# Moving the start addresses of the weight buffers and the stationary activations by two paddings

## The chip, the cores and the metric

The kernel runs on one core of a Trainium2 chip. The metric is the device time of that core in microseconds. Before the change it is 2356.5 us, the median of 3 runs (2355.69 to 2361.19 us).

## The reference

The program is one inference step of a two-layer hybrid backbone (D_MODEL 2048) on two sequences of 128 tokens, a "prompt" and a "sample". Everything is float32. A layer does, cut to what matters here:

```python
h = rms_norm(x, norm_w) * (1 + scale) + shift          # shift, scale, gate = silu(c) @ w_mod + b_mod
(hg..., at..., s5_u, s5_g, merge_raw) = split_columns(h @ w_in)
o_hg = hgrn_branch(...)      # gated linear recurrence, chunkwise
o_at = block_attention(...)  # grouped-query attention
o_s5 = s5_branch(...)        # state space scan, then gelu(y), y * sigmoid(y @ w_glu)
merged = g_hg * (o_hg @ w_br_hg) + g_at * (o_at @ w_br_at) + g_s5 * (o_s5 @ w_br_s5)
x = x + gate * (merged @ w_out)
```

Nearly all the arithmetic is in the products with `w_in`, `w_br`, `w_out` and `w_glu`: for 256 rows (both sequences); the weights come in 672 pieces of 512 KB.

## The kernel before

**The big products.** `gemm` takes pieces of a weight matrix of 256 rows by 512 columns. Each piece lands by DMA (issued from SP) in one of three `raw` buffers. It holds two K-tiles of 128x512. Per K-tile ScalarE writes the rounded copy `wh` (line 138, type float32r) and VectorE the rest `wl = raw - wh` (line 139). Four `wh` and four `wl` buffers go round. The activations were split in the same way, once, into a high and a low part. For each K-tile and each of the two sequences TensorE then does three products into one PSUM tile `g`:

```python
nc.tensor.matmul(ps[s], lo(k)[:, sl], wh, start=(k == 0), stop=False)   # L178
nc.tensor.matmul(ps[s], hi(k)[:, sl], wh, start=False, stop=False)      # L179
nc.tensor.matmul(ps[s], hi(k)[:, sl], wl, start=False, stop=(k == nk - 1))  # L180
```

The activation block (128x128, 512 bytes in each partition) is the stationary operand, loaded into the array by a LDWEIGHTS (PEld). The weight tile (128x512, 2048 bytes in each partition) is the moving operand that streams through. So 1344 K-tiles make 8064 such products, and each of them has a load of its own stationary block.

**Where the operands lie.** The stationary parts have different names and homes. `hh` and `hl` (the normed input, for all of `w_in`) are in four buffers of the tag H8. `oh` and `ol` (outputs of the three branches, for `w_br`) are in two buffers of Z8. `ghl` (for `w_glu`) and one half of `mt` (merged, for `w_out`) are in S16; the other half of `mt` is in H8. The moving parts are always `wh` and `wl`. Every tile is written at a fixed byte address that is the same in all 128 partitions.

**What sets the addresses.** Three pools lie one behind the other: `const` (tables, in the order of their first use), `weights` (`raw`, `wh`, `wl`), and `sb` (all else: k2, Z8, sm, gt, mo, Bl, S16, ys, k4, H8, q4, kv, st and the small ones of the S5 branch). Within a pool each tag has its buffers in a row. A tile that grows by some bytes pushes all behind it up by so many. `c` (line 202) is the first tile of `const`; `bm` (line 251) is the only buffer of the tag mo, between gt and Bl.

**The order of the work.** A scheduler with priorities lays down each engine's list when the program is built. Side work (the S5 scan on VectorE, the `w_mod` products of line 273, attention and the recurrence) is mixed between the big products.

Of the kernel before, what the change touches and what calls it, by code (L numbers as in the profile page):

```python
# [57 lines left out]
def view(t, off, dims):  # L58
    return bass.AP(t.tensor, t.offset + off, [list(t.ap[0])] + [list(d) for d in dims])


class Builder:
# [136 lines left out]

    def condition(self):  # L200
        nc = self.nc
        c = self.const("c", (128, 32), src=self.io["cT"], eng=nc.scalar)
        self.cT = self.const("cs", (128, 64))
        nc.gpsimd.memset(self.cT, 0.0)
        sg = self.t2("sg", (128, 32))
        nc.scalar.activation(sg, c, AF.Sigmoid)
        nc.vector.tensor_mul(self.cT[:, 0:32], c, sg)
# [36 lines left out]
    def mod_part(self, l, part, prio, tags, plan):  # L244

        nc, io = self.nc, self.io
        with self.prio(prio):  # L250
            bm = self.t("mo", "bm", (128, 256))
            src = io["b_mod"][l, part]
            nc.gpsimd.dma_start(bm, bass.AP(src.tensor, src.offset, [[256, 4], [0, 32], [1, 256]]))
        kb = 0
        for bank, run, burst in plan:
            ps = None
            for k0 in range(kb, kb + run, burst):
                ws = []
                for k in range(k0, k0 + burst):
                    with self.prio(P_TOP):  # L260
                        tag, n = next(tags)
                        for i in range(0, 2, n):
                            w = self.t(tag if isinstance(tag, str) else tag[i], "wm", (128, n * 1024))
                            nc.sync.dma_start(w, io["w_mod"][l, part, k][:, i * 1024:(i + n) * 1024])
                            ws += [w[:, j * 1024:(j + 1) * 1024] for j in range(n)]
                with self.prio(prio):
                    if ps is None:
                        pool = dict(g=self.pg, m=self.pm, b=self.pb)[bank]
                        ps = pool.tile([128, 512], F32, tag=bank, name=self.nm("mod"))
                    for j, k in enumerate(reversed(range(2 * k0, 2 * (k0 + burst)))):  # L270
                        for i in range(4):
                            with self.prio(P_MIX if j + i else prio):
                                nc.tensor.matmul(ps[32 * i:32 * i + 32, 0:256], self.cT[:, 2 * k:2 * k + 32],  # L273
                                                 ws[k - 2 * k0][:, i * 256:i * 256 + 256], start=(k0 == kb and j == 0),
                                                 stop=(k0 + burst == kb + run and j == 2 * burst - 1),
                                                 tile_position=(0, 32 * i))
                    if k0 + burst == kb + run:
                        nc.vector.tensor_add(bm, bm, ps[:, 0:256])
                if k0 + burst < 8:
                    yield True  # L280
            kb += run
        with self.prio(P_CHAIN):
            if part >= 4:
                for i in range(4):
                    dst = bass.AP(self.gate_d.tensor, self.gate_d.offset + l * 2 * D + (part - 4) * 1024 + i * 256,
                                  [[D, 2], [1, 256]])
                    nc.gpsimd.dma_start(dst, bm[32 * i:32 * i + 2])
            else:
                tr = self.transpose4(bm, 2)
                mt = self.cp.tile([128, 2, 2, 4], F32, tag=f"modT{part}", name=self.nm("modT"))  # L290
                for s in range(2):
                    nc.vector.tensor_copy(view(mt, s * 4, [[8, 2], [2, 2], [1, 2]]),
                                          view(tr, s, [[64, 2], [32, 2], [128, 2]]))
                nc.vector.scalar_tensor_tensor(mt[:, 1], mt[:, 1], 1.0,
                                               view(self.normw, l * 16 + part * 4, [[0, 2], [1, 4]]), ALU.add, ALU.mult)
                self.mods[part] = mt
        yield True
# [910 lines left out]
```

## Time and profile before

| | |
|---|---|
| median of 3 runs | 2356.5 us |
| profiled execution | 2357.62 us, of which the span of the trace is 2355.8 us |
| TensorE matmul (PE) | busy 2290.3 us, 97% |
| weight load (PEld) | busy 1818.4 us, 77% |
| VectorE (DVE) | busy 1805.0 us, 77% |
| ScalarE (ACT) | busy 1180.3 us, 50% |
| DMA | 483.85 MB, mean 205 GB/s |
[...]

A matmul's own duration (about 0.39 us) is longer than the distance from its start to the next one's start, since matmuls are pipelined and their ends are modelled. What a stream of matmuls costs is therefore the time from the first start to the start of what follows, divided by their number.

### The profile page before, as it was taken

How to read it: one execution, taken by the hardware profiler on the slowest of the kernel's cores; microseconds unless marked ns; L12 is line 12 of the kernel's file. 1: busy time of each engine (PE TensorE's matmuls, PEld its weight loads, DVE VectorE, ACT ScalarE, POOL GpSimd, SP SyncE). 2: the span in 40 equal slices, each digit the busy share in tenths (PEclk: the TensorE clock that was granted, in tenths of full speed). 3: DMA queues.
4: the chain of work that ended last, by engine and by line, in shares of the span. 5: the costliest groups of instructions: out<-in, count | busy, mean ns of one | idle time of the engine just before them, and what ended most of it. 6: DMA issues, size and time to landing. Idle time of an engine off the chain costs nothing.

```text
span 2355.8 us, 38207 instructions
## 1 busy us (share of the span) xinstructions
PE 2290.3 (97%) x13192; PEld 1818.4 (77%) x13192; DVE 1805.0 (77%) x4835; ACT 1180.3 (50%) x2061; POOL 133.7 (6%) x244
## 2 busy tenths in 40 slices
PE   4999999999999999999989999999999999999997
PEld 2767877888887777777767888888878877887876
DVE  5855899799879868765565798899959959956555
ACT  3536645555554344544446555555564544554444
POOL 2000000100000100000010001000010010000000
PEclk8999999999999999999999999999999999999999
DMA  8994554345557878678873554444546577556665
GB/s 312 342 337 134 160 173 137 111 157 183 178 161 247 297 263 311 209 250 273 291 237 129 165 173 150 133 153 152 188 148 193 195 237 246 188 171 224 233 198 177
DMA packets 131490, 483.85 MB, mean 205 GB/s; under 512 B 17200, under 2 KB 17808, under 8 KB 126944
## 3 DMA queue, kind: packets, MB, share of 16 engines
q1 hardware_dynamic: 120528, 454.09, 57.1%
q0 software_dynamic: 9472, 23.97, 3.3%
q10 hardware_dynamic: 1296, 3.36, 0.4%
q8 instruction: 103, 1.69, 0.3%
q14 instruction: 91, 0.75, 0.1%
HBM read 474.36 MB, written 6.98 MB: 204 GB/s over the span
## 4 chain that ended last, share of the span: by engine, by line
PE 90%; DMA 5%; DVE 4%; issue 1%; ACT 1%; SPq 0%; DVEq 0%; ACTq 0%
PE g L178 25%; PE g L180 25%; PE g L179 25%; PE mod L273 3%; PE bu L815 2%; DMA wm<-w_mod 2%; PE lv L431 2%; PE tr L134 2%; DMA raw<-w_in 1%; PE yp L846 1%; DVE wl L139 1%; DMA raw<-w_br 1%; PE yp L839 1%; PE bt L733 1%; PE ao L571 0%
## 5 line engine op out<-in xcount | busy, mean ns | idle before, releaser
L138 ACT CAST wh<-raw 128x512 fp32r<-128x512 f32 x1344 | 819.1, 621 | 948.7 <-PE g L179 625.8
L139 DVE TENSOR_TENSOR wl<-raw,wh 128x512 fp32r<-128x512 f32 x1344 | 915.4, 689 | 382.2 <-ACT wh L138 345.0
L178 PE MATMUL g<-wh,hl 128*128 128x512 f32 x1984 | 794.4, 400 | 5.3 <-ACT wh L138 2.5
L179 PE MATMUL g<-wh,hh 128*128 128x512 f32 x1984 | 787.5, 397 | 0.0
L180 PE MATMUL g<-wl,hh 128*128 128x512 f32 x1984 | 709.8, 402 | 0.1
L178 PEld LDWEIGHTS g<-wh,hl 128*128 128x128 f32 x1984 | 375.0, 189 | 105.4 <-ACT wh L138 7.8
L179 PEld LDWEIGHTS g<-wh,hh 128*128 128x128 f32 x1984 | 375.2, 189 | 83.1 <-issue 0.2
L180 PEld LDWEIGHTS g<-wl,hh 128*128 128x128 f32 x1984 | 368.5, 189 | 87.7 <-DVE wl L139 2.9
L178 PE MATMUL g<-wh,ol 128*128 128x512 f32 x384 | 151.8, 395 | 0.8 <-ACT wh L138 0.6
L827 DVE TENSOR_TENSOR p<-s5sc,Sb 128x64 f32<-128x64 f32 x512 | 140.6, 275 | 15.0 <-ACT Sb L819 5.9
L179 PE MATMUL g<-wh,oh 128*128 128x512 f32 x384 | 150.0, 391 | 0.0
L833 DVE TENSOR_TENSOR Sb<-Sb,p 128x64 f32<-128x64 f32 x512 | 141.5, 276 | 8.9
L829 DVE TENSOR_TENSOR p<-s5sc,Sb 128x64 f32<-128x64 f32 x512 | 138.8, 271 | 0.0
L180 PE MATMUL g<-wl,oh 128*128 128x512 f32 x384 | 132.1, 393 | 0.0
L273 PE MATMUL mod<-wm,cs 128*32 128x256 f32 x1536 | 103.5, 401 | 24.9 <-DMA wm<-w_mod 18.5
L832 DVE TENSOR_TENSOR p<-p,p 128x64 f32<-128x64 f32 x512 | 113.3, 221 | 6.1
L273 PEld LDWEIGHTS mod<-wm,cs 128*32 128x32 f32 x1536 | 44.2, 113 | 76.0 <-DMA wm<-w_mod 23.7
L178 PE MATMUL g<-wh,mt 128*128 128x512 f32 x256 | 101.5, 397 | 0.0
L179 PE MATMUL g<-wh,mt 128*128 128x512 f32 x256 | 101.0, 394 | 0.0
L178 PEld LDWEIGHTS g<-wh,ol 128*128 128x128 f32 x384 | 72.1, 188 | 18.1 <-ACT wh L138 2.1
L180 PE MATMUL g<-wl,mt 128*128 128x512 f32 x256 | 84.7, 398 | 1.2 <-DVE wl L139 1.2
L180 PEld LDWEIGHTS g<-wl,oh 128*128 128x128 f32 x384 | 71.7, 188 | 16.6 <-DVE wl L139 0.8
(315 smaller groups left out, 2117.0 us busy)
## 6 DMA issues: line engine op xcount, KB each, us to landing
raw<-w_in SPq DMA_DIRECT2D x496, 512.0 KB, 3.6
wm<-w_mod SPq DMA_DIRECT2D x130, 512.0 KB, 7.1
raw<-w_br SPq DMA_DIRECT2D x96, 512.0 KB, 4.2
raw<-w_out SPq DMA_DIRECT2D x64, 512.0 KB, 4.3
wm<-w_mod SPq DMA_DIRECT2D x31, 1024.0 KB, 7.5
raw<-w_glu SPq DMA_DIRECT2D x16, 512.0 KB, 3.5
gb<-gate_d POOLq DMA_DIRECT2D x16, 256.0 KB, 5.9
x<-x ACTq DMA_DIRECT2D x2, 1024.0 KB, 14.5
```

Source lines behind the costliest of these rows:

```text
L134: nc.tensor.transpose(ps[:, k], src[:, k * 128:(k + 1) * 128], self.ident)
L138: self.nc.scalar.copy(hi, src)
L139: self.nc.vector.tensor_sub(lo, src, hi.bitcast(F32))
L178: nc.tensor.matmul(ps[s], lo(k)[:, sl], wh, start=(k == 0), stop=False)
L179: nc.tensor.matmul(ps[s], hi(k)[:, sl], wh, start=False, stop=False)
L180: nc.tensor.matmul(ps[s], hi(k)[:, sl], wl, start=False, stop=(k == nk - 1))
L273: nc.tensor.matmul(ps[32 * i:32 * i + 32, 0:256], self.cT[:, 2 * k:2 * k + 32], ws[k - 2 * k0][:, i * 256:i * 256 + 256], start=(k0 == kb ...
L431: nc.tensor.matmul(ps[:, h], mix[:, h], view(Z, HT + h * 128, [[2 * m, nb], [2 * HT + m, 2], [1, m]]), start=True, stop=True)
L827: tt(p0.rearrange("p d (j s) -> p d j s", s=2), view(sc, qd * 32, [[16, 2], [1, 16], [0, 2]]), view(Sb, i, [[ds, 2], [2 * W, 16], [W, 2]]) ...
L829: tt(p1, view(sc, 128 + qd * 64, [[32, 2], [16, 2], [1, 16]]), view(Sb, i + RI, [[ds, 2], [-RI, 2], [W, 16]]), ALU.mult)
L832: tt(p0, p0, p1, ALU.add)
L833: tt(cur, cur, p0, ALU.add)
```

## The change

Two tiles get wider, and only their first columns are used. `c` has 80 columns in place of 32, which is 192 bytes more; its load by DMA is written out on a line of its own. `bm` has 352 columns in place of 256, which is 384 bytes more. All tiles behind `c` move up by 192 bytes, all behind `bm` by 576.

```diff
     def condition(self):
         nc = self.nc
-        c = self.const("c", (128, 32), src=self.io["cT"], eng=nc.scalar)
+        c = self.const("c", (128, 80))[:, 0:32]
+        nc.scalar.dma_start(c, self.io["cT"])
         self.cT = self.const("cs", (128, 64))
...
         with self.prio(prio):
-            bm = self.t("mo", "bm", (128, 256))
+            bm = self.t("mo", "bm", (128, 352))[:, 0:256]
             src = io["b_mod"][l, part]
             nc.gpsimd.dma_start(bm, bass.AP(src.tensor, src.offset, [[256, 4], [0, 32], [1, 256]]))
```

The addresses of the two built programs, as bytes in a partition (the first buffer of each; a stationary block steps by 512 bytes within its tile, a buffer by 2048 or more, so the last two columns hold for every block of the row):

| tag | what | before | after | before mod 512 | after mod 512 |
|---|---|---|---|---|---|
| ident | identity, moving operand of the transposes | 16896 | 17088 | 0 | 192 |
| raw | weights as landed | 27968 | 28160 | 320 | 0 |
| wh, wl | moving operands | 40256, 48448 | 40448, 48640 | 320 | 0 |
| k2 | 2 KB work tiles | 56640 | 56832 | 320 | 0 |
| Z8 | `oh`, `ol`, `x`, `Z` | 68928 | 69120 | 320 | 0 |
| gt | gates, `hf` | 86464 | 86656 | 448 | 128 |
| mo | `bm` | 94656 | 94848 | 448 | 128 |
| Bl | S5 input matrices | 95680 | 96256 | 448 | 0 |
| S16 | `ghl`, half of `mt`, S5 states `Sb` | 103872 | 104448 | 448 | 0 |
| ys, k4, H8, q4, kv, st | H8: `hh`, `hl`, half of `mt` | 140992 (H8) | 141568 (H8) | 192 | 256 |

The instructions of each engine stand in the same order before and after, with the same waits; none is added, removed or moved. Only the source line of the load of `c` is another one.

## Rows read from the trace of the kernel before

**Rows 1.** The page: busy time of each engine, its share and its instructions.
```profile
PE 2290.3 (97%) x13192; PEld 1818.4 (77%) x13192; DVE 1805.0 (77%) x4835; ACT 1180.3 (50%) x2061; POOL 133.7 (6%) x244
```

**Rows 2.** The page: the chain that ended last, share by engine.
```profile
PE 90%; DMA 5%; DVE 4%; issue 1%; ACT 1%; SPq 0%; DVEq 0%; ACTq 0%
```

**Rows 3.** Timeline of PE from 2001 us: start us, us, what.
```profile
2001.28 0.40 PE L178 MATMUL g<-wh,hl 128*128 128x512 f32 x1
...
2023.60 0.40 PE L178 MATMUL g<-wh,ol 128*128 128x512 f32 x1
...
2034.52 0.40 PE L178 MATMUL g<-wh,hl 128*128 128x512 f32 x1
```

**Rows 4.** Groups of PE, 2001.3 to 2023.5 us; xcount | busy us, mean ns | idle.
```profile
L178 PE MATMUL g<-wh,hl 128*128 128x512 f32 x32 | 12.6, 395 | 0.0
L179 PE MATMUL g<-wh,hh 128*128 128x512 f32 x32 | 12.6, 395 | 0.0
L180 PE MATMUL g<-wl,hh 128*128 128x512 f32 x32 | 10.0, 394 | 0.0
```

**Rows 5.** Groups of PE, 2023.7 to 2034.2 us.
```profile
L178 PE MATMUL g<-wh,ol 128*128 128x512 f32 x16 | 6.2, 390 | 0.0
```

**Rows 6.** Timeline of PE around the w_glu product of layer 1.
```profile
2129.27 0.39 PE L178 MATMUL g<-wh,ghl 128*128 128x512 f32 x1
...
2146.71 0.27 PE L134 MATMUL tr<-ident,glu 128*128 128x128 f32 x1
```

**Rows 7.** Groups of PE, 2129.3 to 2146.4 us.
```profile
L178 PE MATMUL g<-wh,ghl 128*128 128x512 f32 x25 | 9.9, 394 | 0.0
```

**Rows 8.** Groups of the whole run, shapes apart.
```profile
L178 PE MATMUL g<-wh,hl 128*128 128x512 f32 x1984 | 794.4, 400 | 5.3 <-ACT wh L138 2.5 <-DVE hl L139 1.8 <-ACT ff L385 0.8
L178 PE MATMUL g<-wh,ol 128*128 128x512 f32 x384 | 151.8, 395 | 0.8 <-ACT wh L138 0.6
L178 PE MATMUL g<-wh,mt 128*128 128x512 f32 x256 | 101.5, 397 | 0.0
L178 PE MATMUL g<-wh,ghl 128*128 128x512 f32 x64 | 25.2, 394 | 0.0
L139 DVE TENSOR_TENSOR wl<-raw,wh 128x512 fp32r<-128x512 f32 x1344 | 915.4, 689 | 382.2 <-ACT wh L138 345.0 <-PE g L180 20.4 <-PE g L179 6.0
L139 DVE TENSOR_TENSOR hl<-hf,hh 128x512 fp32r<-128x512 f32 x16 | 11.1, 691 | 6.8 <-ACT hh L138 6.8
L138 ACT CAST hh<-hf 128x512 fp32r<-128x512 f32 x16 | 9.9, 620 | 12.3 <-DVE hf L327 12.1
L138 ACT CAST wh<-raw 128x512 fp32r<-128x512 f32 x1344 | 819.1, 621 | 948.7 <-PE g L179 625.8 <-DMA raw<-w_in 117.4 <-DVE wl L139 60.4
L555 PE MATMUL sc<-kT,qT 128*128 128x256 f32 x32 | 8.2, 379 | 0.0
```

**Rows 9.** Timeline of PE in the attention of layer 0.
```profile
326.88 1.02 PE L555 MATMUL sc<-kT,qT 128*128 128x256 f32 x4
```

**Rows 10.** Stretches of 60 us: busy us (x) by engine, PEclk, DMA share, GB/s.
```profile
60.00:120.00 60.00, 60.00 (x384) 41.79 (x383) 50.83 (x258) 29.41 (x55) 1.56 (x4) 1.00 0.92 341
480.00:540.00 60.00, 60.00 (x307) 50.72 (x306) 57.90 (x149) 33.36 (x57) 0.00 (x0) 1.00 0.47 149
1980.00:2040.00 60.00, 60.00 (x262) 48.96 (x261) 57.65 (x173) 28.74 (x49) 0.00 (x0) 1.00 0.60 193
```

**Rows 11.** Groups of PE from 0 to 180 us.
```profile
L178 PE MATMUL g<-wh,hl 128*128 128x512 f32 x144 | 59.0, 410 | 0.3 <-DVE hl L139 0.3
```

**Rows 12.** Timeline of PE around 2330 us (the w_out product of layer 1).
```profile
2319.53 0.40 PE L178 MATMUL g<-wh,mt 128*128 128x512 f32 x1
...
2330.73 0.40 PE L178 MATMUL g<-wh,mt 128*128 128x512 f32 x1
```

**Rows 13.** Groups of PE, 2319.6 to 2330.6 us.
```profile
L178 PE MATMUL g<-wh,mt 128*128 128x512 f32 x16 | 6.4, 398 | 0.0
```

## The prediction

> **What bounds the kernel now.** I read the busy times first: TensorE works 2290.3 us of a span of 2355.8 us, and no other engine is over 77% [rows 1]. The chain that ended last agrees: 90% of it is PE, 5% DMA, 4% VectorE [rows 2]. So a change that moves no instruction can matter in three places only: how far apart TensorE's products stand, how long VectorE and ScalarE take for one instruction, and how fast DMA fills the buffers.
>
> Then I read how far apart the products stand. From the first `hl` product at 2001.28 us to the first `ol` product at 2023.60 us there are 96 products [rows 3, 4] with nothing between them: 22.32 us / 96 = 232.5 ns each. From there to the next `hl` product at 2034.52 us there are 48 [rows 3, 5]: 10.92 / 48 = 227.5 ns. [...] Is it the form of the product, eight K-tiles for `ol` and sixteen for `hl`? The `w_glu` product has eight as well, and takes 75 products from 2129.27 to 2146.71 us [rows 6, 7]: 17.44 / 75 = 232.5 ns. So eight K-tiles do not make it fast. What differs is where the stationary block lies. By the table of addresses, `oh` and `ol` start at 320 mod 512 as `wh` and `wl` do. `hh` and `hl` (192) and `ghl` (448) lie 128 bytes off them, to one side and to the other. The reader is to see that the distance between two products follows the address: with equal remainders 5.0 ns less than 128 bytes apart. Nearly every product has its 128 bytes now: L178 stands with 1984 for `hl`, 256 for `mt` and 64 for `ghl` against 384 for `ol` [rows 8], and each of these counts three times, for L178 to L180.
>
> **The change part by part.** *The distance between products.* H8 holds the operand of 1984 x 3 = 5952 products of `w_in` and of half of the 256 x 3 = 768 of `w_out`: 6336. S16 holds the other 384 and the 192 of `w_glu`: 576. Z8 holds 384 x 3 = 1152. After the change `wh` and `wl` are at 0, Z8 and S16 at 0, H8 at 256. Equal remainders mod 512 are therefore certain for Z8 (as before) and S16 (new). H8 goes from 128 apart to 256 apart, which no tile has before. It is equal mod 256, and the trace gives no row for it. The bounds, from the nearest rows: 227.5 ns if what counts is the remainder mod 256, 232.5 ns if only equality mod 512 helps; and further out, 214 ns if starting at such a multiple removes the whole loss, and some 237.5 ns if 256 apart costs twice what 128 apart does. The 214 comes from four 128x256 f32 products in a row that take 1.02 us with a last duration of 379 ns [rows 8, 9]: (1020 - 379) / 3; it is the shortest distance that an instruction of about this length shows. I take 227.5 for H8, since the two directions of 128 (192 and 448 against 320) cost the same 5.0 ns, which is what a pattern that repeats every 256 bytes gives.
>
> The sum: in the first 180 us, where DMA is 92% busy at 341 GB/s [rows 10], a shorter product only waits longer for weights. So the 144 x 3 = 432 products there [rows 11] count nothing (2.2 us if they did). H8: (6336 - 432) x 5.0 ns = 29.5 us. S16: 576 x 5.0 = 2.9 us. Z8: 0. Together 32.4 us on the engine that sets the end. A product that follows other work of TensorE, or a wait, does not have the full 5 ns to give back, and I take off some 2 us for these: 30 us.
>
> *What is late next.* TensorE would be 2.1% faster in its products. Where VectorE is fullest it has 57.90 of 60 us [rows 10]; 2.1% less time makes that 57.9 of 58.7, still not full. ScalarE waits for PE 625.8 us before `wh` [rows 8], and that wait only gets shorter. So the gain should stay.
>
> *VectorE and ScalarE.* Their operands move too. `wl` from `raw` and `wh`, all three equal mod 512, takes 689 ns; `hl` from `hf` and `hh`, 448 against 192, takes 691. The casts take 621 (`wh`) and 620 (`hh`) [rows 8]. No address shows in them: 0, with an end of 2 ns x 1344 = 2.7 us either way, off the path.
>
> *The small products and the transposes.* `ident` leaves a multiple of 512 for 192. Products of f32 show no loss to begin with: the four of [rows 9] have their stationary and moving tiles (k4 at 192, k2 at 320) 128 apart and still stand 214 ns from each other. I take 0; some 600 transposes at 5 ns would be 3 us either way.
>
> *DMA.* The rows of `raw` land at 0 in place of 320. No two transfers of the trace differ in this alone. DMA has 5% of the chain, 118 us [rows 2]; if it went by the same 2.1%, that would be 2.5 us either way. I take 0. [...]
>
> The profiled execution took 2357.6 us, of which 1.8 us lie outside the span, and is 1.1 us over the median of 2356.5. So 2357.6 - 30 = 2327.6, and against the median some 2327.
>
> **The rivals.**
>
> *Only equality mod 512 helps.* Then S16 alone gains, 2.9 us: 2354 us. For it: the one fast case in the trace is equal mod 512, and H8 will not be. Against it: nothing but the symmetry of 192 and 448, which a pattern of 512 can have as well. 14%.
>
> *The start itself counts.* If loads and streams that start at a multiple of 256 lose nothing, all products come nearer to 214 ns. Halfway, at 221 ns: (5904 + 576) x 11.5 ns + 1152 x 6.5 ns = 82 us, 2275 us. All the way it would be twice that less what VectorE then holds up: in a stretch such as 480 to 540 us it has only 2.1 us of 60 to give [rows 10], and PE would want up to 8%, 4.8 us. For it: even the fast case stands 13.5 ns over 214. Against: the same operand at 64 and at 192 mod 256 differs by only 5 ns, and both are off such multiples. 16%.
>
> *Slower: 256 apart is worse than 128.* The place is H8, 5904 products on the path. The worst steady state of the trace is 48 `mt` products in S16 from 2319.53 to 2330.73 us [rows 12, 13], 11.20 / 48 = 233.3 ns, so equal addresses already give more than one state. If 256 apart costs twice the 5.0 ns, H8 stands at 237.5: 5904 x 5.0 - 2.9 = 26.6 us more, 2383 us. It decides from 232.5 + (7.1 + 2.9) us / 5904 = 234.2 ns. 13%.
>
> *The address is not the cause.* Z8 may be fast for another reason, for instance who wrote it or what runs beside it; then nothing changes, 2357 us. Against it: the 5 ns come and go at the very product where the tile changes, in both directions [rows 3]. [...] 7%.
>
> **How the numbers follow.** The forecast (H8 and S16 as Z8) has 50%. What a measurement of this kernel can tell from no change is 0.3%, 7 us. Faster: forecast and "the start itself", 66%, and 1% for a part of the gain in the first rival: 67%. Same: the rest of the first rival and the last: 20%. Slower: 13%. The range of 8 in 10 reaches down past the halfway case's upper half, to 2280 us, and up over the two cases of no change to the lower part of the slower one, 2368 us. The forecast's own range is 2318 to 2340 us.
>
> **What would show it.** In the profile after: the distance of `hl` products in an unmixed stretch (232.5 to about 227.5 ns; 232.5 means the first rival or the last, over 234.2 the slower one, under 225 the start itself); of `ghl` products (227.5 unless the address is not the cause); of `ol` products (227.5 unless the start counts); PE's busy time lower by about 30 us at the same instructions; means of L138 and L139 within 2 ns of 621 and 689; `raw` landing as before. I am wrong if `ghl` gets faster and `hl` does not, or if PE's busy time falls and its idle time rises by as much.

## The result and the profile after

The changed kernel takes 2332.7 us, the median of 5 runs (2331.86 to 2334.85), against 2356.73 us (2355.69 to 2361.19) of the kernel before on the same chip: a ratio of 0.9894, 95% interval 0.9880 to 0.9908. It is 24 us faster. The forecast was 2327 us, with a range of 2280 to 2368. The profiled execution took 2331.88 us, its span 2330.1 us.

The page of the kernel after has, of busy times and of the chain:

```profile
PE 2257.9 (97%) x13192; PEld 1812.2 (78%) x13192; DVE 1798.2 (77%) x4835; ACT 1180.8 (51%) x2061; POOL 133.9 (6%) x244
...
PE 82%; DVE 8%; DMA 7%; issue 2%; ACT 1%; SPq 0%; POOL 0%; DVEq 0%; ACTq 0%; POOLq 0%
```

Against [rows 1] PE is busy 32.4 us less with the same 13192 instructions, and no other engine moved by more than 7 us. Against [rows 2] the chain has less PE and more VectorE and DMA, and PE's idle time, span less busy time, has gone from 65.5 to 72.2 us: it waits a little more for others.

The stream of products, in the same place of the program as [rows 3]; this is PE's timeline after (start us, us, what):

```profile
1981.88 0.39 PE L178 MATMUL g<-wh,hl 128*128 128x512 f32 x1
...
2003.64 0.39 PE L178 MATMUL g<-wh,ol 128*128 128x512 f32 x1
...
2014.52 0.39 PE L178 MATMUL g<-wh,hl 128*128 128x512 f32 x1
```

96 products of `hl` and `hh` in 21.76 us are 226.7 ns each, where it was 232.5. The 48 of `ol` and `oh` behind them take 10.88 us, 226.7 ns too, where it was 227.5. The border that stood at 2023.60 us before has gone. The trace before also has 48 products of `ol` and `oh` that stand closer than those 227.5 ns:

```profile
2204.50 0.39 PE L178 MATMUL g<-wh,ol 128*128 128x512 f32 x1
...
2215.39 0.40 PE L178 MATMUL g<-wh,hl 128*128 128x512 f32 x1
```

10.89 us / 48 = 226.9 ns: these stood nearly where all stand now. The `w_glu` product after, to be held against [rows 6]:

```profile
2107.08 0.39 PE L178 MATMUL g<-wh,ghl 128*128 128x512 f32 x1
...
2124.09 0.27 PE L134 MATMUL tr<-ident,glu 128*128 128x128 f32 x1
```

75 products in 17.01 us, 226.8 ns for 232.5. The groups of the whole run after, shapes apart, for [rows 8] (xcount | busy us, mean ns | idle before):

```profile
L178 PE MATMUL g<-wh,hl 128*128 128x512 f32 x1984 | 785.1, 396 | 6.4 <-ACT wh L138 2.7 <-DVE hl L139 2.0 <-ACT ff L386 1.5
L178 PE MATMUL g<-wh,ol 128*128 128x512 f32 x384 | 152.0, 396 | 2.5 <-ACT wh L138 2.3
L139 DVE TENSOR_TENSOR wl<-raw,wh 128x512 fp32r<-128x512 f32 x1344 | 915.5, 689 | 368.5 <-ACT wh L138 319.1 <-PE g L179 21.4 <-PE g L180 20.2
L139 DVE TENSOR_TENSOR hl<-hf,hh 128x512 fp32r<-128x512 f32 x16 | 11.1, 696 | 6.7 <-ACT hh L138 6.7
L138 ACT CAST wh<-raw 128x512 fp32r<-128x512 f32 x1344 | 819.4, 622 | 925.0 <-PE g L179 459.8 <-DVE wl L139 194.8 <-DMA raw<-w_in 113.5
```

VectorE's 689 ns and ScalarE's 622 ns are the same as before; `hl` on its 16 instructions went from 691 to 696. ScalarE's wait for PE fell from 625.8 to 459.8 us, but its wait for VectorE (`wl`) rose from 60.4 to 194.8; both together fell from 686.2 to 654.6 us, so the weights have a little less of a lead. In the stretch that the prediction watched for VectorE, it now has 58.58 us of 60 where it had 57.90 [rows 10]:

```profile
480.00:540.00 60.00, 60.00 (x312) 51.55 (x311) 58.58 (x150) 31.63 (x54) 0.00 (x0) 1.00 0.50 156
```

### The profile page after: what moved, and what is told of

Its sections match the earlier page's. It is cut to its first block, busy times and chain, and to the rows that moved or that the text cites. A ratio compares the mean times of both kernels' runs of the same rounds, so it can differ in the third digit from the quotient of the medians.

```text
span 2330.1 us, 38207 instructions
## 1 busy us (share of the span) xinstructions
PE 2257.9 (97%) x13192; PEld 1812.2 (78%) x13192; DVE 1798.2 (77%) x4835; ACT 1180.8 (51%) x2061; POOL 133.9 (6%) x244
## 4 chain that ended last, share of the span: by engine, by line
PE 82%; DVE 8%; DMA 7%; issue 2%; ACT 1%; SPq 0%; POOL 0%; DVEq 0%; ACTq 0%; POOLq 0%
PE g L178 23%; PE g L180 23%; PE g L179 22%; DMA raw<-w_in 3%; DVE wl L139 3%; PE mod L274 3%; PE bu L816 3%; PE lv L432 2%; DMA raw<-w_br 2%; DMA wm<-w_mod 2%; PE tr L134 2%; PE yp L847 1%; DVE p L830 1%; DVE Sb L834 1%; ACT wh L138 1%
## 5 line engine op out<-in xcount | busy, mean ns | idle before, releaser
L138 ACT CAST wh<-raw 128x512 fp32r<-128x512 f32 x1344 | 819.4, 622 | 925.0 <-PE g L179 459.8
L178 PE MATMUL g<-wh,hl 128*128 128x512 f32 x1984 | 785.1, 396 | 6.4 <-ACT wh L138 2.7
L179 PE MATMUL g<-wh,hh 128*128 128x512 f32 x1984 | 777.9, 392 | 0.0
L180 PE MATMUL g<-wl,hh 128*128 128x512 f32 x1984 | 700.9, 398 | 0.4 <-DVE wl L139 0.3
L180 PEld LDWEIGHTS g<-wl,oh 128*128 128x128 f32 x384 | 71.5, 188 | 17.6 <-DVE wl L139 2.4
```

Of the source, the lines that this page charges most:

```text
L138: self.nc.scalar.copy(hi, src)
```

## The experiments

All twelve are variants of these two kernels. Their times are set against the kernel before, run on the same chip. For the distance I take the same 96 products of layer 1 each time, from the first `hl` to the first `ol` behind them. In this stretch PE is busy throughout (22.32 of 22.32 us before, 21.76 of 21.76 after) and the granted clock is 1.00 in both, so neither idle time nor the clock makes that difference; the clock's mean over the whole run is 0.992 before, 0.994 after and 0.990 to 0.995 in the variants.

**One padding alone: is it the remainder of one operand against the other, or the multiple?**

```diff
-        c = self.const("c", (128, 80))[:, 0:32]
-        nc.scalar.dma_start(c, self.io["cT"])
+        c = self.const("c", (128, 32), src=self.io["cT"], eng=nc.scalar)
```

> Only bm is widened (384 bytes). The weight buffers stay at 320 mod 512, H8 comes to 64, S16 to 320: the remainders mod 256 of stationary and moving operand are equal (64 and 64), but nothing starts at a multiple of 256. Theory A (the remainder of one against the other, mod 256, decides): hl products 227.8 ns apart, ghl 227.0, PE busy near 2258 us, time 2333 us as in the full change. Theory B (the start at a multiple of 256 decides): hl stays at 232.5 ns, time 2354 to 2357 us.

Measured: 2335.15 us, ratio 0.9893 (0.9879 to 0.9908). Its timeline of PE:

```profile
1984.51 0.39 PE L178 MATMUL g<-wh,hl 128*128 128x512 f32 x1
...
2006.27 0.39 PE L178 MATMUL g<-wh,ol 128*128 128x512 f32 x1
```

21.76 us / 96 = 226.7 ns, as after the change, with every operand at 64 mod 256. Theory A holds, theory B falls.

The other padding alone:

```diff
-            bm = self.t("mo", "bm", (128, 352))[:, 0:256]
+            bm = self.t("mo", "bm", (128, 256))
```

> Only c is widened (192 bytes). raw, wh, wl and Z8 begin at multiples of 512 as after the change, H8 at 384 and S16 at 128, 128 off the weight buffers as before. Theory A (relative remainder): hl 232.5 ns, ol 227.5, time 2357 us, no change. Theory B (start at a multiple): part of the gain, hl between 227.8 and 232.5 ns and ol under 227.5, time 2335 to 2350 us.

Measured: 2359.49 us, ratio 0.9999 (0.9990 to 1.0008).

```profile
2003.15 0.40 PE L178 MATMUL g<-wh,hl 128*128 128x512 f32 x1
...
2025.46 0.40 PE L178 MATMUL g<-wh,ol 128*128 128x512 f32 x1
```

22.31 / 96 = 232.4 ns. With `raw`, `wh`, `wl` and Z8 at multiples of 512 nothing is gained: not in the products, and not by DMA into `raw` either. The whole gain belongs to `bm`'s 384 bytes, because they lie between the moving and most of the stationary operands. The padding of `c` shifts both together and does nothing that can be measured.

**Other distances.** `bm` gets another width in place of 352, `c` stays as before the change.

```diff
-            bm = self.t("mo", "bm", (128, 352))[:, 0:256]
+            bm = self.t("mo", "bm", (128, 304))[:, 0:256]
```

That is 64 apart; 272 columns give 192, 296 give 32, 280 give 224 and 264 give 160.

> bm 192 bytes wider, c as before: H8 at 384, S16 at 128, weight buffers at 320 mod 512, so that stationary and moving operand are 64 apart mod 256. Theory A in its simplest form (only equality mod 256 helps): 232.5 ns, 2357 us. Rival A2 (the cost grows with the distance, up to 128): some 230 ns, 2345 us. Rival A3 (a block of 64 bytes is what repeats): 227.8 ns, 2333 us.

> bm 64 bytes wider, c as before: H8 at 256, S16 at 0, weight buffers at 320 mod 512, so that the stationary operand is 192 behind the moving one mod 256 (64 to the other side). Theory A: 232.5 ns, 2357 us. A2 (by distance, either side): as with 64 apart, some 230 ns, 2345 us. [...] Theory B (start of the stationary tile at a multiple of 256): 227.8 ns, 2333 us.

> bm 160 bytes wider, c as before: H8 at 352, S16 at 96, weight buffers at 320 mod 512, so the stationary operand is 32 ahead of the moving one mod 256. The distances measured so far are 227.8 ns (0 apart), 233.3 (64), 232.5 (128), 229.3 (192). Theory A with a lopsided curve (a stationary block that lies ahead costs, one behind costs less): between 230 and 234 ns, PE busy 2275 to 2294 us. Rival A3 (a 64 byte unit counts, so that 32 is as 0 or as 64): 227.8 or 233.3 ns.

> bm 96 bytes wider, c as before: H8 at 288, S16 at 32, weight buffers at 320 mod 512: 32 behind, 224 mod 256. Theory A with its least at equality: between 227.8 and 229.3 ns, time 2333 to 2345 us. Rival (the least of the curve lies a little behind equality): under 227.5 ns and under 2330 us.

> bm 32 bytes wider, c as before: H8 at 224, S16 at 480, weight buffers at 320 mod 512, the stationary operand 160 ahead mod 256. Between the points 128 (232.5 ns) and 192 (229.3): if only 0 and 192 are good places (32, 64, 128 and 224 all stand at 232.5 to 233.3), 233 ns and no change in time; if there is a slope from 128 to 192, near 231 ns and 2350 us.

The timelines of PE, 64 apart and then 192 apart:

```profile
2003.38 0.40 PE L178 MATMUL g<-wh,hl 128*128 128x512 f32 x1
...
2025.78 0.39 PE L178 MATMUL g<-wh,ol 128*128 128x512 f32 x1
```

```profile
1995.00 0.39 PE L178 MATMUL g<-wh,hl 128*128 128x512 f32 x1
...
2016.97 0.39 PE L178 MATMUL g<-wh,ol 128*128 128x512 f32 x1
```

And 32, 160 and 224 apart, in this order:

```profile
2009.25 0.39 PE L178 MATMUL g<-wh,hl 128*128 128x512 f32 x1
...
2031.65 0.39 PE L178 MATMUL g<-wh,ol 128*128 128x512 f32 x1
...
2001.66 0.39 PE L178 MATMUL g<-wh,hl 128*128 128x512 f32 x1
...
2024.05 0.40 PE L178 MATMUL g<-wh,ol 128*128 128x512 f32 x1
...
2002.33 0.39 PE L178 MATMUL g<-wh,hl 128*128 128x512 f32 x1
...
2024.72 0.39 PE L178 MATMUL g<-wh,ol 128*128 128x512 f32 x1
```

| stationary ahead of moving, mod 256 | 0 | 32 | 64 | 128 | 160 | 192 | 224 |
|---|---|---|---|---|---|---|---|
| ns from product to product, the same 96 | 226.7 | 233.3 | 233.3 | 232.5 | 233.3 | 228.9 | 233.2 |
| time, us | 2335.15 | 2365.93 | 2365.03 | 2360.82 | 2358.26 | 2344.32 | 2362.07 |
| ratio to before on its chip | 0.9893 | one run | 1.0018 | 1 | one run | 0.9926 | 1.0008 |

The column 0 is the run with `bm` alone, the column 128 the kernel before beside it. 64 apart is slower than before by an interval of 1.0007 to 1.0030; 224 apart is 0.9997 to 1.0018, no difference shown. So A2, a cost that grows with the distance, is wrong: 32 bytes are as bad as 160 in the distance between products. (Of the 7.7 us between the times of these two single runs, 6.8 lie in one stretch that is looked at below, 555.66 against 548.88 us; there the trace at 32 has PE idle for 5.3 us more, waiting.) A3 is wrong too, since 64 is not as 0. Theory A, that only equality helps, misses one point: 192 apart has two thirds of the gain, 228.9 ns and 0.9926 (0.9908 to 0.9944). Theory B expected 227.8 ns and 2333 us there, which is not what came. But this run is also the only one in which the stationary tiles start at a multiple of 256 and the moving ones do not, so that its part of the gain may come from either; the runs do not tell these apart. At 224 both of my expectations missed: they were 229.3 ns or less, and 233.2 came.

In the same five traces the 48 `ol` products behind, whose tag Z8 lies ahead of `bm` and keeps its place to `wh` and `wl`, stand 226.7 to 227.7 ns apart. The curve is flat at some 233 ns with one deep place and one shallow one. 96 was not tried, nor any offset that isn't a multiple of 32.

**Half a stationary block: do the two reads collide?** All products but those of the first and last K-tile of a group use 64 of the 128 columns.

```diff
-                        nc.tensor.matmul(ps[s], lo(k)[:, sl], wh, start=(k == 0), stop=False)
+                        full = k in (0, nk - 1)
+                        sl = sl if full else slice(s * 128, s * 128 + 64)
+                        o = ps[s] if full else ps[s][0:64]
+                        nc.tensor.matmul(o, lo(k)[:, sl], wh, start=(k == 0), stop=False)
...
```

> Addresses as before the change; all products but those of the first and the last K-tile of a group load a stationary block of 64 columns (256 bytes in a partition) in place of 128 and write 64 partitions, so the results are not the reference's. The moving operand and the number of products stay. Theory E (what the address costs is the reading of the stationary block against that of the moving one): with half the bytes to read, the loss over 214 ns falls, from 18.5 to some 9 ns, hl products near 223 ns, and so does the loss by the address. Rival (the address counts once per product, whatever is loaded): 232.5 ns.

> The same with the addresses of the change. Theory E: the loss over 214 falls from 13.5 to some 7 ns, hl near 221 ns, 2 to 3 ns under the run with the addresses of before. Rival: 227.8 ns, 5 ns under it.

Measured: 2349.75 us with the addresses of before, 2352.33 us with those of after, one run each. The timelines, first before, then after:

```profile
1995.70 0.40 PE L181 MATMUL g<-wh,hl 128*128 128x512 f32 x1
...
2017.76 0.39 PE L181 MATMUL g<-wh,ol 128*128 128x512 f32 x1
```

```profile
1999.09 0.39 PE L181 MATMUL g<-wh,hl 128*128 128x512 f32 x1
...
2021.13 0.39 PE L181 MATMUL g<-wh,ol 128*128 128x512 f32 x1
```

22.06 and 22.04 us for 96, 229.8 and 229.6 ns. These 96 are mixed: the first six and the last six, of the first and the last K-tile, still have whole blocks. The 84 between them have half blocks alone; here are the first product after the first six and the first of the last six, before and then after:

```profile
1997.09 0.40 PE L181 MATMUL g<-wh,hl 128*64 128x512 f32 x1
...
2016.36 0.39 PE L181 MATMUL g<-wh,hl 128*128 128x512 f32 x1
...
2000.45 0.40 PE L181 MATMUL g<-wh,hl 128*64 128x512 f32 x1
...
2019.77 0.39 PE L181 MATMUL g<-wh,hl 128*128 128x512 f32 x1
```

The half blocks stand 19.27 us / 84 = 229.4 ns apart with the addresses of before and 19.32 / 84 = 230.0 with those of the change; the last six, whole blocks, take 1.40 and 1.36 us, 233 and 227 ns, as in the full kernels. So the address still counts for the whole blocks and no longer for the half ones. That excludes the rival, by which the half blocks had to stay at 232.5 and 227.8 ns. Theory E is not borne out: the distance does not come down to 223 or 221 ns, and with the addresses of the change the half block is even slower than the whole one, 230.0 against 226.7 ns. But it is not excluded either. The half products also write 64 partitions in place of 128, so more than the read has changed; something that these runs do not name holds them at some 230 ns, and a gain below that could not show.

**Where the rest of the saved time went.** In the merge stage of layer 0, each `w_mod` part loads its first quarter of weights only, so PE does the same products with fewer loads.

```diff
                 for k in range(k0, k0 + burst):
+                    if few and k0 > 0:
+                        ws = kept
+                        continue
                     with self.prio(P_TOP):
```

> Addresses as before the change. In the merge stage of layer 0 each w_mod part loads only the first quarter of its weights and uses it four times: 18 of each 24 of those loads are left out, so that the results of these modulations are not the reference's; TensorE does the same products. DMA should fall from some 0.8 to 0.6 in that stage. The stage loses some waits: 2345 to 2357 us.

> The same left out, with the addresses of the change. Theory D (the 6 to 7 us of the 32 that did not reach the end were lost where late weights end PE's waits, between 700 and 1240 us): the distance to the run with the addresses of before grows from 24 to 30 us or more, and TensorE saves some 7 us in that stage, where it saved 3 with all loads. Rival (they were lost to VectorE or at the joints of the products all over the run): the distance stays at 24 to 26 us.

Measured: 2351.37 us (0.9955, 0.9937 to 0.9974) and 2321.14 us (0.9832, 0.9814 to 0.9851), 30.2 us apart where the two kernels with all loads are 24.0 apart. The intervals alone do not part 30 from 24. The traces show where it is, by the start of the same two instructions: an `ol` product (the first of the fourth group of 48 in layer 0), shortly before the `w_mod` products of this stage begin, and a transpose of `xn` (the 25th of the 32 of layer 1), after they have ended. All loads, before:

```profile
710.07 0.40 PE L178 MATMUL g<-wh,ol 128*128 128x512 f32 x1
...
1260.26 0.27 PE L134 MATMUL tr<-ident,xn 128*128 128x128 f32 x1
```

All loads, after:

```profile
702.45 0.39 PE L178 MATMUL g<-wh,ol 128*128 128x512 f32 x1
...
1249.81 0.27 PE L134 MATMUL tr<-ident,xn 128*128 128x128 f32 x1
```

Few loads, addresses of before:

```profile
710.17 0.40 PE L178 MATMUL g<-wh,ol 128*128 128x512 f32 x1
...
1253.56 0.27 PE L134 MATMUL tr<-ident,xn 128*128 128x128 f32 x1
```

Few loads, addresses of after:

```profile
703.08 0.39 PE L178 MATMUL g<-wh,ol 128*128 128x512 f32 x1
...
1240.71 0.27 PE L134 MATMUL tr<-ident,xn 128*128 128x128 f32 x1
```

With all loads this stretch takes 550.19 us before and 547.36 after: 2.8 us saved. With few loads it is 543.39 and 537.63: 5.8 us. Each of these is one profile, and the stretch varies: with all loads it took 548.88 to 549.49 us in the runs with `c` alone and with 64, 160 and 224 apart, 553.52 and 555.66 with 192 and 32, and 547.98 with `bm` alone. Steadier is what PE does in it. Its busy time falls by 6.5 us with all loads (536.02 to 529.55) and by 6.2 with few (532.23 to 525.99). Its idle time rises from 14.2 to 17.8 us with all loads (from 14.1 to 17.6 between the run with `c` alone and that with `bm` alone), and with few loads only from 11.2 to 11.6. What PE waited for weights from 700 to 1240 us, all loads before and then all loads after (us in total, times, longest):

```profile
PE mod L273 <- DMA wm<-w_mod: 2.4, 3, 1.8
PE g L178 <- ACT wh L138: 1.3, 1, 1.3
PE g L180 <- DVE wl L139: 1.2, 2, 0.8
```

```profile
PE mod L274 <- DMA wm<-w_mod: 3.5, 3, 1.9
PE g L178 <- ACT wh L138: 2.6, 3, 1.5
PE g L180 <- DVE wl L139: 2.5, 4, 1.0
```

These three rise from 4.9 to 8.6 us. The DMA share of this stage, all loads after and few loads after (columns: stretch, busy us of PE, PEld, DVE, ACT and POOL, PEclk, DMA share, GB/s):

```profile
700.00:1240.00 540.00, 522.74 (x3170) 404.46 (x3168) 386.88 (x971) 240.57 (x416) 37.59 (x66) 0.99 0.75 260
```

```profile
700.00:1240.00 540.00, 528.36 (x3213) 412.87 (x3212) 395.95 (x989) 250.84 (x430) 36.97 (x66) 0.99 0.59 193
```

So here a good half of what the faster products saved ran into weights that were not there yet. Theory D holds in this stage, as far as single profiles show it; the fewer loads were expected to give back some 4 us and gave 2.9.

**Spreading those loads.**

```diff
-MRATE = (0.36, 0.13)
+MRATE = (0.33, 0.13)
```

> The changed kernel with one number more: the w_mod side work of layer 0's merge stage goes at a rate of 0.33 in place of 0.36, so that its 24 portions are spread over some 145 pieces of weights in place of 133 (of 152). Theory D (late weights take back part of the gain there): DMA in the fullest stretches falls by some 3%, and PE gets back 1 to 3 of the 5 us that it does not gain in that stage: ratio to the kernel before 0.988 to 0.989, 2 us under the change, hardly more than the interval. Rival (the waits there come from single late pieces, whatever the rate): the same as the change, 0.9894.

Measured: 2336.67 us, ratio 0.9905 (0.9889 to 0.9921): no better than the change. PE's same waits from 700 to 1240 us, to be held against those of the change above:

```profile
PE mod L274 <- DMA wm<-w_mod: 7.6, 6, 4.1
PE g L178 <- ACT wh L138: 1.2, 2, 0.7
PE g L180 <- DVE wl L139: 1.9, 3, 1.0
```

The `w_mod` products wait more, 7.6 for 3.5 us, the big products less, 3.1 for 5.1; together it is 10.7 for 8.6. The time fits the rival, that the waits come from single late pieces whatever the rate, but the DMA share of this stretch has not fallen (0.76 for 0.75), so the run hardly tests theory D and does not show why the pieces are late. No version here beats the change.

## Why the prediction was right, and where it was off

*What bounds the kernel.* Right: PE, by the distance from product to product.

*The distance between products.* Right in sign, place and size. H8, 256 apart, which no row of before showed, behaves as Z8. The size was a little low: I had taken 227.5 ns, a saving of 5.0, and the unmixed stretch has 226.7, a saving of 5.8. The row that I took it from has the border in it; the other stretch of `ol` before, at 226.9 ns, was nearer. Neither the instruction nor the clock sets the two stretches of [rows 3] apart: 128x512 in both [rows 4, 5], granted 1.00 [rows 10]. The reason that I gave, a pattern of 256, was borne out as far as 0 and 256 are alike; that 32, 64, 160 and 224 are all as bad as 128 I could not know, and that both sides of 128 cost the same proves little on such a curve.

*The sum.* 32.4 us on PE were forecast, and PE's busy time fell by 32.4 us (2290.3 to 2257.9). That agreement is chance in part. 6480 products at 5.8 ns would have been 37.6 us, and the 432 products of the first 180 us, which I left out, are in the measured number: 32.4 us over all 6912 is 4.7 ns each, so the products between other work must have given less than 5.8. So errors of opposite sign met.

*What is late next.* This step was too small. I said that the gain should stay, but for 2 us, and watched VectorE for it. The span fell by 25.7 us; 6.7 of the 32.4 came back as idle time of PE. More than half of this, 3.6 us, lies in one stage. Of the (340 + 128 + 32) x 3 = 1500 products of H8 and S16 between the two marks I had counted 7.5 us; PE's busy time there fell by 6.5, and the stage gave 2.8. There the DMA share is 0.75. I had taken such products out of the sum in the first 180 us, where it is 0.92 from 60 to 120 us, and should have asked the same of the next fullest stage. VectorE, at 58.58 of 60, did hold.

*The parts at nothing.* `raw` at 0 in place of 320 brought nothing that could be measured (0.9999, 0.9990 to 1.0008, padding of `c` alone). Casts and subtractions stood at their 622 and 689 ns.

*The rivals.* Equality mod 512 alone is excluded by H8's 226.7 ns. The start itself, as the cause of this gain, is excluded by the run with `bm` alone, which has all of the gain and starts none of these operands at a multiple of 256; for the part at 192 apart it stays possible. That the address is not the cause is excluded by that run beside the kernel before, which differ in addresses only. One instruction stands 226.7 or 233.3 ns from the next by its addresses alone. The slower rival did not come true 256 apart, but distances that cost more than 128 exist: 64 apart is slower than before (1.0007 to 1.0030).

*What stays open.* Why a product stands 226.7 ns from the next at equal remainders and some 233 else. The half blocks, at some 230 ns with either addresses, do not settle it.

## What to carry to other kernels

When one instruction stands at two different distances in the trace, ask where its operands lie: here the remainder of the stationary against the moving operand, mod 256 bytes, was worth 2.5% of a float32r product in an unmixed stretch (226.7 ns for 232.5), and one unused stripe of 384 bytes between two tiles gave all of it. Pad what lies between the two operands, not what lies ahead of both (here a ratio of 0.9893 against 0.9999). And where DMA is as busy as it was here in layer 0's merge stage, at 0.75, expect less of the gain: here 2.8 us of the 7.5 counted, while PE's waits for weights rose from 4.9 to 8.6 us.

## What the runs showed that I had not expected

- The curve over the distance is no slope. From 0 to 32 bytes it steps from 226.7 to 233.3 ns, and at 192 it dips to 228.9, where the start of the stationary tiles may play a part.
- A stationary block of 64 columns makes the product slower than one of 128 at the good addresses, 230.0 against 226.7 ns, and the addresses then no longer matter much, 229.4 against 230.0.
